# Attention's order of work: copies that follow one another at the rate of issue, and two weight tiles fetched at the head of the stage

## The chip, the cores and the metric

One core of a Trainium2 chip runs the whole model in one launch. The core has a matrix engine (PE, TensorE; its weight loads are shown as PEld), a vector engine (DVE), an activation engine (ACT), GpSimd (POOL) and SyncE (SP), which here mostly issues DMA transfers. Each engine takes its instructions strictly in the order in which the program lists them; engines wait for one another by semaphores. The metric is device time in microseconds for one execution, 2202.79 us before the change, the median of three runs.

## The reference

The input has 1024 tokens of width 1024. Layer 0 mixes tokens with a gated linear recurrence, layer 1 with stick-breaking attention, and each is followed by a SwiGLU feed-forward block. The change touches only the attention of layer 1:

```python
qkv = einsum("bsd,de->bse", rms_norm(h), w_qkv)       # q, k, v of 16 heads of 64
z = einsum("bhqd,bhkd->bhqk", q, k) / 8
log_fail = where(s < t, log_sigmoid(-z), 0)           # strictly earlier keys only
suffix = reversed_cumsum(log_fail) - log_fail
weights = where(s < t, exp(log_sigmoid(z) + suffix), 0)
out = einsum("bhqk,bhkd->bhqd", weights, v) @ w_o     # then the residual and the FFN
```

## The kernel before, in words

Values are float32. Each operand of a matrix product is split into a high part, rounded to the matrix engine's format, and a low part, the remainder; a product is then three matmuls (high by high, low by high, high by low; `mm3`, lines 443 to 446), or two where one side is held exactly.

Attention works on eight pairs of heads, because two heads of 64 fill the 128 partitions. For each pair q there are six projection groups: Q, K and V (`which` = 0, 1, 2), each for the two halves n of the tokens. A group is eight steps `proj` (`project`, line 1709) of three 512-column matmuls each. For Q and K the result is scaled by DVE into `t` (`scaled`, L1723), split by ACT into `qh` (`q_hi`, L1727) and by DVE into `ql` (`q_lo`, L1731), and then copied by DMA to other partitions: `move` (L1746) copies 64 rows by 512 columns, four times for a Q group and eight for a K group. Of the eight copies of a K group, x = 0 to 3 are for the first head (`kh` twice, then `kl` twice) and x = 4 to 7 for the second. A step `z` (`z_part`, L1786) multiplies a 128-token block of Q with `kh` and with `kl`; ACT takes the sigmoid into `F` (L1798), DVE the running product (L1805, L1807). PE transposes the result (`T`, L1817), ACT and DVE split it (L1822, L1826), and PE multiplies it with V (`av`, L1834). V itself is differenced and transposed as `vt` (L1757) and split (L1768, L1772). There are 24 `z` chunks and 24 units of `T` and `av` in a pair; a head's chunks begin with the blocks j = 0 to 3 of the first half and go on with j = 4 to 7, whose diagonal chunks need the second K group (n = 1).

Weights for a projection come from HBM into one of three `raw` buffers (`load_raw`, L425, 512 KB each), and are split by ACT and DVE in two halves (`whi` L1697, `wlo` L1701). All of these transfers, the copies, the weights, the stores `out` of finished heads (L1895) and, for the last pair, the loads `back` of those (L1775) are issued by SP, in one queue.

The order of the instructions on every engine is not written by hand. `attention_plan` (line 191) adds tasks to a `Plan` (line 35), each with an engine, an assumed duration, its dependencies and a rank (a due time in units). `Plan.emit` then runs a list scheduling: it repeatedly takes the ready task that could begin first, the lower rank deciding ties, and emits it. What it assumes of time changes only the order in which instructions are listed; what makes an engine wait in the execution are the real dependencies. A DMA task in the plan keeps the queue for 0.55 and ends after its own duration (line 68):

```python
            if eng == "dma":
                free[eng], end[i] = begin + 0.55, begin + us
```

In the plan before, each copy of a group also depends on the copy before it (`m`), so that eight copies follow one another at the full duration of 2.1 plus 0.15. Nothing in the kernel's data asks for that; SP issues the copies as they come in its list.

Ahead of the plan stands a loop written out by hand (lines 1911 to 1933): it issues the projections (0,0,n) and (0,1,n), that is Q and K of the first pair, and at the head of each weight's first group it loads a further one: weight (0,1) at g = 0, weight (0,2) at g = 2, after the copies of group (0,0,1). The splits of the loaded weight follow PE's steps one by one from the list `later`. The plan begins where this loop ends, with the times of the engines given as `Plan(pe=0.0, dve=1.0, act=1.0, dma=1.0)`.

Of the kernel before, what the change touches and what calls it, by code (L numbers as in the profile page):

```python
# [190 lines left out]
def attention_plan(plan, fn):  # L191
    NP, LEAD = HEADS // 2, 8
# [4 lines left out]
    chunks, units = [], []  # L197
    for q in range(NP):
# [5 lines left out]
        else:  # L204
# [3 lines left out]
            for h in heads:  # L208
                chunks += diag(h, range(4, NT)) + rest(h)
                units += upper(h)  # L210
    mm = lambda n: n / 2400 + 0.008
    act = lambda n: 0.08 + n * 0.00082
    dve = lambda n: 0.07 + n * 0.00103

    wlo, wraw, wuse = {}, {}, {}

    def weights(i, name, r, raw, use):
        ld = plan.add("dma", 2.6, fn["load", name], [raw], r - 4)
        h0 = plan.add("act", 0.5, fn["whi", name, 0], [ld, use], r - 2.5)
        l0 = plan.add("dve", 0.6, fn["wlo", name, 0], [h0], r - 2.3)  # L220
        h1 = plan.add("act", 0.5, fn["whi", name, 1], [h0], r - 2.1)
        wlo[name] = (l0, plan.add("dve", 0.6, fn["wlo", name, 1], [h1, l0], r - 1.9))
        wraw[i] = wlo[name][1]
# [3 lines left out]
    vadd, kept, zlast, avlast, vlow, turn = {}, {}, {}, {}, {}, {}  # L227
    is_kept = lambda q, n: q < NP - 2 + (n == 0)
    order = []
    for i, (q, which, n) in enumerate(groups):  # L230
        s, wi = 24 * (q - 1) + 4 * (i % 6), 3 * q + which
        if i >= 4:
            if n == 0 and wi > 2:
                weights(wi, (q, which), s, wraw.get(wi - 3), wuse.get(wi - 2))
            p = None
            for k in range(ND):
                need = [p, pt.get(i - 2) if k == 0 else None]
                if wi > 2:
                    need.append(wlo[q, which][k // 4])
                p = plan.add("pe", 0.692, fn["proj", q, which, n, k], need, s + k / 2 + 0.5)  # L240
            proj[i] = wuse[wi] = p
        s += 4
        if i < 3:
            continue
        p = proj.get(i)
        if which < 2:
            order.append(i)
            was = order[-3] if len(order) > 2 else None
            pt[i] = plan.add("dve", 0.6, fn["t", q, which, n], [p, moves.get(was)], s + 0.1)
            th = plan.add("act", 0.5, fn["qh", q, which, n], [pt[i], moves.get(was)], s + 0.2)  # L250
            tl = plan.add("dve", 0.6, fn["ql", q, which, n], [th], s + 0.3)
            m = None
            for x in range(4 + 4 * which):
                src = (tl if x % 2 else th) if which == 0 else (tl if x // 2 % 2 else th)
                old = [(zlast, q - 2)] if q > 1 else []
                m = plan.add("dma", 2.1, fn["move", q, which, n, x], [src, m, *old], s + 0.4)
                moved[q, which, n, x // (2 + 2 * which)] = m
            moves[i] = m
        else:
            old = [(vadd, (q - 2, x)) for x in range(2)] if q > 1 else []  # L260
            pt[i] = plan.add("dve", 0.6, fn["t", q, which, n], [p, *old], s + 0.1)
            before = (dv, (q, n - 1) if n else (q - 1, 1)) if q or n else None
            turned = (turn, (q, n - 1) if n else (q - 1, 1)) if q or n else None
            dv[q, n] = plan.add("dve", 0.66, fn["dv", q, n], [pt[i], before, turned], s + 0.4)
            if q == NP - 1:
                m = None
                for y in range(NP - 1 - n):
                    for x in range(2):
                        m = plan.add("dma", 2.4, fn["back", y, n, x], [p, (kept, (y, n)), m], s + 0.5)
                        back[y, n] = m  # L270

    sig, scan, T = {}, {}, {}
    users = {}
    for c, (q, hx, j, ci) in enumerate(chunks):
        s, dg = c - LEAD, j // 4 == ci
        n = (j % 4 + 1) * P if dg else NB
        need = [sig.get(c - 2), moved.get((q, 0, j // 4, hx)), moved.get((q, 1, ci, hx))]
        zlast[q] = zz = plan.add("pe", 2 * mm(n), fn["z", c], need, s)
        if q < NP - 1:
            f = j if dg else j + 4  # L280
        elif dg:
            f = j % 4 + 4 * hx
        else:
            f = j + 4 + 4 * hx
        free = [(T, u) for u in users.get(f, ())] + ([(zlast, NP - 2)] if f >= 12 else [])
        sig[c] = plan.add("act", act(n), fn["sig", c, f], [zz, *free], s + 0.2)
        need = [sig[c], None if dg else scan[q, hx, j, 1]]
        scan[q, hx, j, ci] = plan.add("dve", 0.07 + n * 0.00222, fn["scan", c], need, s + 0.3)
        users[f] = [
            u for u, (q_, hx_, G, kb) in enumerate(units)  # L290
            if (q_, hx_, G) == (q, hx, j // 4) and kb // 4 == ci and kb <= j
        ]

    turns = {}
    for q in range(NP):
        first = [u for u, x in enumerate(units) if x[0] == q]
        turns[max(first[0] - 1, 0)] = (q, 0)
        turns[next(u for u in first if units[u][3] >= 4) - 1] = (q, 1)
    tl, av, ring, banks, sums = {}, {}, [], [], {}
    stored = None  # L300
    for u, (q, hx, G, kb) in enumerate(units):
        if u in turns:
            v = turns[u]
            old = [(avlast, v[0] - 2)] if v[0] > 1 else []
            turn[v] = t = plan.add("pe", 0.45, fn["vt", *v, len(ring)], [dv[v], *ring[-2:-1]], u - 1.9)
            vh = plan.add("act", 0.5, fn["vh", *v], [t, *old], u - 1.8)
            vlow[v] = plan.add("dve", 0.6, fn["vl", *v], [vh], u - 1.7)
            ring.append(vlow[v])
        js = range(max(kb, 4 * G), 4 * G + 4)
        n = len(js) * P  # L310
        need = [scan[q, hx, j, kb // 4] for j in js] + ring[-2:-1]
        T[u] = plan.add("pe", 0.109 * len(js) + 0.02, fn["T", u, len(ring)], need, u - 1.8)
        th = plan.add("act", act(n), fn["th", u], [T[u], av.get(u - 3)], u - 1.6)
        tl[u] = plan.add("dve", dve(n), fn["tl", u], [th], u - 1.5)
        ring.append(tl[u])
        need = [tl[u], av.get(u - 1), (vlow, (q, kb // 4)), *(banks[-2:-1] if kb == 4 * G else ())]
        av[u] = plan.add("pe", 2 * mm(n), fn["av", u, len(banks)], need, u + 0.8)
        if kb != 3:
            continue
        avlast[q] = av[u]  # L320
        s = u + 1
        need = [av[u], sums.get((q, G)) if hx else kept.get((q - 1, G))]
        g0 = plan.add("act", 0.5, fn["g0", q, hx, G], need, s)
        g1 = plan.add("dve", 0.6, fn["g1", q, hx, G], [g0], s + 0.1)
        banks.append(g1)
        sums[q, G] = g1
        if hx == 0:
            continue
        vadd[q, G] = plan.add("dve", 0.66, fn["vadd", q, G], [g1, pt.get(6 * q + 4 + G)], s + 0.5)
        free = stored if is_kept(q, G) else proj[len(groups) - 2 + G]  # L330
        ph = plan.add("act", 0.5, fn["ph", q, G], [vadd[q, G], free], s + 0.6)
        kept[q, G] = plan.add("dve", 0.66, fn["pl", q, G], [ph], s + 0.7)
        if is_kept(q, G):
            stored = plan.add("dma", 2.1, fn["out", q, G, 0], [ph], s + 0.8)
            kept[q, G] = plan.add("dma", 2.1, fn["out", q, G, 1], [kept[q, G], stored], s + 0.9)

    s, out = 24 * (NP - 1), []
    for o in range(4):
        i = 3 * NP + o
        weights(i, f"o{o}", s + 6 * o - 2, wraw.get(i - 3), wuse.get(i - 2) if o < 2 else zlast[NP - 2])  # L340
        p = None
        bank = pt[len(groups) - 2 + o] if o < 2 else out[o - 2]
        for k in range(ND):
            need = [p, bank, wlo[f"o{o}"][k // 4], back[k, 0] if k < NP - 1 else kept[NP - 1, 0]]
            p = plan.add("pe", 0.685, fn["ob", o, k], need, s + 4 * o + k / 2 + 0.6)
        if o < 2:
            out.append(plan.add("act", 0.5, fn["keep", o], [p, pt[len(groups) - 2 + o]], s + 4 * o + 5))
# [4 lines left out]
def trunk(  # L352
# [1309 lines left out]
    with ExitStack() as st:  # L1662
# [201 lines left out]
        def ob_part(o, k):  # L1864
# [2 lines left out]
            product(OB[o], f"o{o}", k, 0)  # L1867

        acts = {
            "load": load,  # L1870
            "whi": w_hi,
            "wlo": w_lo,
# [35 lines left out]
        E = mybir.EngineType  # L1908
        with tc.manual_schedule(engines={E.PE, E.Activation, E.DVE, E.Pool, E.SP}):
            sts, later = stats_steps(), []  # L1910
            for i in range(4 * ND):
                if i >= 5:
                    next(sts, None)
                g, k = divmod(i, ND)
                if k == 0:
# [6 lines left out]
                            move(*was, x)  # L1922
                    if g % 2 == 0:
                        name = (0, g // 2 + 1)
                        load(name)
                        later += [
                            lambda a=name: w_hi(a, 0),
                            lambda a=name: (w_lo(a, 0), w_hi(a, 1)),
# [2 lines left out]
                project(0, g // 2, g % 2, k)  # L1931
                if i >= 5 and later:
                    later.pop(0)()
            plan = Plan(pe=0.0, dve=1.0, act=1.0, dma=1.0)
            chunks, units = attention_plan(plan, Steps(acts))
            plan.emit()
            mix.load(2)
# [59 lines left out]
```

## Time and profile before

| | us |
|---|---|
| median of 3 runs (lowest, highest) | 2202.79 (2198.71, 2205.09) |
| the profiled execution | 2201.81 |
| its span, first to last instruction | 2200.0 |
| attention, from the first projection to the last product of the plan | about 950 to 1480 of the span |
| one pair of heads in the middle of attention | about 61 |

A stretch of the span given as A:B is in microseconds from the first instruction. A row of a timeline gives start, duration, engine, line and what is written and read; in brackets, where there is one, the engine's idle time before it and what ended that. For SP the duration of a merged row also holds its waits. The duration of a matmul row holds its passage through the array; the distance from one start to the next tells how fast they follow.

### The profile page before, as it was taken

To read this page: it belongs to the slowest core of one execution; us is meant where nothing else is said; L and a number is where in the kernel's file an instruction comes from. 1 tells how busy PE (TensorE), PEld (TensorE's weight loads), DVE (VectorE), ACT (ScalarE), POOL (GpSimd) and SP (SyncE) were. 2 spreads that over 40 slices of the span, in tenths; PEclk is the share of its full clock that TensorE was granted. 3 is DMA by queue.
4 is the path that set the end of the run, shared out by engine and by line. 5 is a ranking of instruction groups with operands and counts; after the bars stand their busy time and mean duration, and the time that the engine had idled before them with its cause. 6 is when DMAs were issued, how large, how long until landed. Compare 5 with 4: busy or idle time off the path is not lost.

```text
span 2200.0 us, 27262 instructions
## 1 busy us (share of the span) xinstructions
PE 2167.9 (99%) x10054; PEld 1798.9 (82%) x10054; DVE 1709.1 (78%) x2434; ACT 1078.5 (49%) x1776; POOL 35.6 (2%) x44
## 2 busy tenths in 40 slices
PE   9999999999999999989999999999999999999997
PEld 7888888888888888868888888888888888888886
DVE  7978678677777887957888888877876777788886
ACT  5577444444444554644555555544534444454455
POOL 0000010000000000000000000002000000000001
PEclk9999999999999999989999999999999999999999
DMA  4111312344444864433333333442133444466442
GB/s 174 39 48 48 125 39 91 98 138 139 150 146 130 286 197 129 128 102 108 99 94 94 91 101 97 136 178 88 58 115 117 149 136 149 153 236 225 134 138 87
DMA packets 132598, 274.50 MB, mean 125 GB/s; under 512 B 15344, under 2 KB 22640, under 8 KB 132464
## 3 DMA queue, kind: packets, MB, share of 16 engines
q1 hardware_dynamic: 132032, 271.97, 38.9%
q8 instruction: 79, 1.29, 0.2%
q10 hardware_dynamic: 432, 0.79, 0.1%
q14 instruction: 55, 0.45, 0.1%
HBM read 176.75 MB, written 70.78 MB: 113 GB/s over the span
## 4 chain that ended last, share of the span: by engine, by line
PE 90%; DVE 5%; ACT 2%; DMA 2%; issue 1%; SPq 0%; DVEq 0%; ACTq 0%
PE p_ps L446 18%; PE p_ps L444 18%; PE p_ps L445 18%; PE qk_ps L444 3%; PE qk_ps L445 3%; PE qk_ps L446 3%; PE z_ps L1786 3%; PE a_ps L445 3%; PE a_ps L444 3%; PE a_ps L446 3%; PE av_ps L1834 3%; PE wt_ps L1817 2%; PE ob_ps L444 2%; PE ob_ps L445 2%; PE ob_ps L446 2%; DMA kl<-ql 2%
## 5 line engine op out<-in xcount | busy, mean ns | idle before, releaser
L444 PE MATMUL p_ps<-vh,wbh 128*128 128x512 f32 x524 | 204.9, 391 | 2.0 <-ACT ta L1362 2.0
L446 PE MATMUL p_ps<-vh,wbl 128*128 128x512 f32 x524 | 204.8, 391 | 0.0
L446 PE MATMUL p_ps<-vh,wcl 128*128 128x512 f32 x524 | 204.1, 390 | 0.5 <-DVE wcl L977 0.5
L445 PE MATMUL p_ps<-vl,wbh 128*128 128x512 f32 x524 | 204.6, 390 | 0.0
L446 PE MATMUL p_ps<-vh,wal 128*128 128x512 f32 x524 | 204.1, 389 | 0.1
L444 PE MATMUL p_ps<-vh,wch 128*128 128x512 f32 x524 | 204.1, 389 | 0.0
L445 PE MATMUL p_ps<-vl,wch 128*128 128x512 f32 x524 | 203.9, 389 | 0.0
L445 PE MATMUL p_ps<-vl,wah 128*128 128x512 f32 x524 | 203.9, 389 | 0.0
L444 PE MATMUL p_ps<-vh,wah 128*128 128x512 f32 x524 | 203.8, 389 | 0.0
L1798 ACT ACTIVATE F<-z_ps 128x512 f32<-128x512 f32 (+3 forms) x188 | 91.8, 490 | 168.3 <-PE z_ps L1786 167.2
L963 ACT CAST wbh<-sb 128x1024 fp32r<-128x1024 f32 (+2 forms) x69 | 69.6, 1008 | 192.6 <-DVE sb L947 192.6
L1805 DVE TENSOR_TENSOR_SCAN F<-F,unit 128x128 f32<-128x128 f32 (+3 forms) x128 | 104.8, 821 | 62.9 <-ACT F L1798 62.7
L444 PE MATMUL qk_ps<-vh,whi 128*128 128x512 f32 x264 | 119.4, 452 | 0.7 <-ACT vh L524 0.7
L444 PEld LDWEIGHTS p_ps<-vh,wbh 128*128 128x128 f32 x524 | 98.7, 188 | 22.7 <-ACT ta L1362 2.5
L446 PEld LDWEIGHTS p_ps<-vh,wbl 128*128 128x128 f32 x524 | 98.8, 189 | 21.9 <-DVE wbl L967 1.3
L446 PEld LDWEIGHTS p_ps<-vh,wcl 128*128 128x128 f32 x524 | 98.4, 188 | 21.8 <-DVE wcl L977 1.3
L446 PEld LDWEIGHTS p_ps<-vh,wal 128*128 128x128 f32 x524 | 98.4, 188 | 21.3 <-DVE wal L958 1.0
L445 PEld LDWEIGHTS p_ps<-vl,wbh 128*128 128x128 f32 x524 | 98.7, 188 | 20.4
L445 PEld LDWEIGHTS p_ps<-vl,wah 128*128 128x128 f32 x524 | 98.4, 188 | 20.4
L445 PEld LDWEIGHTS p_ps<-vl,wch 128*128 128x128 f32 x524 | 98.4, 188 | 20.4
L444 PEld LDWEIGHTS p_ps<-vh,wah 128*128 128x128 f32 x524 | 98.4, 188 | 20.3
L444 PEld LDWEIGHTS p_ps<-vh,wch 128*128 128x128 f32 x524 | 98.4, 188 | 20.3
(375 smaller groups left out, 5494.5 us busy)
## 6 DMA issues: line engine op xcount, KB each, us to landing
raw<-in_ffn_w_in SPq DMA_DIRECT2D x88, 512.0 KB, 3.6
vl<-pd SPq DMA_DIRECT2D x128, 256.0 KB, 3.6
pd<-U SPq DMA_DIRECT2D x90, 256.0 KB, 2.3
raw<-in_ffn_w_out SPq DMA_DIRECT2D x28, 512.0 KB, 4.1
raw<-in_attn_w_qkv SPq DMA_DIRECT2D x24, 512.0 KB, 4.4
kh<-qh SPq DMA_DIRECT2D x64, 128.0 KB, 2.3
kl<-ql SPq DMA_DIRECT2D x64, 128.0 KB, 2.7
acc<-pd SPq DMA_DIRECT2D x28, 256.0 KB, 2.6
```

The lines of the kernel that those rows point to most:

```text
L444: nc.tensor.matmul(ps, lhsT=wh, rhs=mh, start=first, stop=False, **kw)
L445: nc.tensor.matmul(ps, lhsT=wh, rhs=ml, start=False, stop=False, **kw)
L446: nc.tensor.matmul(ps, lhsT=wl, rhs=mh, start=False, stop=last, **kw)
L963: nc.scalar.copy(self.full(self.wb), self.full(self.sb))
L1786: nc.tensor.matmul(ps[:, 0:n], lhsT=lhsT, rhs=rhs, start=i == 0, stop=i == 1)
L1798: nc.scalar.activation(F, Z.pop(c)[:, 0:n], AF.Sigmoid, scale=-SC)
L1805: V.tensor_tensor_scan(rev, rev, unit[:, NB - n :][:, ::-1], 0.0, op0=ALU.mult, op1=ALU.add)
L1817: nc.tensor.transpose(tp[:, c : c + P], F[:, (kb % 4) * P : (kb % 4 + 1) * P], ident)
L1834: nc.tensor.matmul(ps[:, c:], lhsT=VV[q][:, kb, hx], rhs=t.pop(u)[:, c:], start=kb == 4 * G and i == 0, stop=kb == 3 and i == 1,)
```

## The change

The change keeps every instruction of the computation and alters what the planner assumes and two places of the hand-written loop.

1. In the plan, copies (`move`), stores (`out`) and loads (`back`) no longer depend on the copy ahead of them, and take 2.4 instead of 2.1. `moved`, `moves` and `back` hold lists, so that what uses a group depends on all its copies.
2. The plan's duration of a weight load is 4.8 instead of 2.6, a projection step 0.705 instead of 0.692, and the constant of a matmul 0.015 instead of 0.008.
3. The transposes `vt` of V are due one unit later.
4. The first K group's copies, made ahead of the plan, are no longer taken as there at once, but at 1.3 and 3.7 (`clock0`, `clock1`, tasks that emit nothing); DVE and ACT start at 0.5 instead of 1.0, the DMA queue at 1.3.
5. In the loop ahead of the plan, the loads of weights (0,1) and (0,2) are both issued at its head. The splits stay where they were.

```diff
@@ attention_plan
-    mm = lambda n: n / 2400 + 0.008
+    mm = lambda n: n / 2400 + 0.015
...
-        ld = plan.add("dma", 2.6, fn["load", name], [raw], r - 4)
+        ld = plan.add("dma", 4.8, fn["load", name], [raw], r - 4)
...
+    for hx in range(2):
+        moved[0, 1, 0, hx] = [plan.add(f"clock{hx}", 1.3 + 2.4 * hx, fn["wait", 0])]
...
-                p = plan.add("pe", 0.692, fn["proj", q, which, n, k], need, s + k / 2 + 0.5)
+                p = plan.add("pe", 0.705, fn["proj", q, which, n, k], need, s + k / 2 + 0.5)
...
-            m = None
+            old = [(zlast, q - 2)] if q > 1 else []
             for x in range(4 + 4 * which):
                 src = (tl if x % 2 else th) if which == 0 else (tl if x // 2 % 2 else th)
-                old = [(zlast, q - 2)] if q > 1 else []
-                m = plan.add("dma", 2.1, fn["move", q, which, n, x], [src, m, *old], s + 0.4)
-                moved[q, which, n, x // (2 + 2 * which)] = m
-            moves[i] = m
+                m = plan.add("dma", 2.4, fn["move", q, which, n, x], [src, *old], s + 0.3 + x / 100)
+                moved.setdefault((q, which, n, x // (2 + 2 * which)), []).append(m)
+                moves.setdefault(i, []).append(m)
...
             if q == NP - 1:
-                m = None
                 for y in range(NP - 1 - n):
-                    for x in range(2):
-                        m = plan.add("dma", 2.4, fn["back", y, n, x], [p, (kept, (y, n)), m], s + 0.5)
-                        back[y, n] = m
+                    back[y, n] = [
+                        plan.add("dma", 2.4, fn["back", y, n, x], [p, (kept, (y, n))], s + 0.5 + y / 10) for x in range(2)
+                    ]
...
-        turns[max(first[0] - 1, 0)] = (q, 0)
-        turns[next(u for u in first if units[u][3] >= 4) - 1] = (q, 1)
+        turns[first[0]] = (q, 0)
+        turns[next(u for u in first if units[u][3] >= 4)] = (q, 1)
...
-            stored = plan.add("dma", 2.1, fn["out", q, G, 0], [ph], s + 0.8)
-            kept[q, G] = plan.add("dma", 2.1, fn["out", q, G, 1], [kept[q, G], stored], s + 0.9)
+            stored = plan.add("dma", 2.4, fn["out", q, G, 0], [ph], s + 0.8)
+            kept[q, G] = plan.add("dma", 2.4, fn["out", q, G, 1], [kept[q, G]], s + 0.9)
@@ trunk, ahead of the plan
             sts, later = stats_steps(), []
+            load((0, 1))
+            load((0, 2))
...
                         name = (0, g // 2 + 1)
-                        load(name)
...
-            plan = Plan(pe=0.0, dve=1.0, act=1.0, dma=1.0)
+            plan = Plan(pe=0.0, dve=0.5, act=0.5, dma=1.3, clock0=0.0, clock1=0.0)
```

More of the change, by code (lines that the diff above doesn't have):

```diff
@@ L248, in attention_plan @@
             was = order[-3] if len(order) > 2 else None
-            pt[i] = plan.add("dve", 0.6, fn["t", q, which, n], [p, moves.get(was)], s + 0.1)
-            th = plan.add("act", 0.5, fn["qh", q, which, n], [pt[i], moves.get(was)], s + 0.2)
+            pt[i] = plan.add("dve", 0.6, fn["t", q, which, n], [p, *moves.get(was, ())], s + 0.1)
+            th = plan.add("act", 0.5, fn["qh", q, which, n], [pt[i], *moves.get(was, ())], s + 0.2)
             tl = plan.add("dve", 0.6, fn["ql", q, which, n], [th], s + 0.3)
-            m = None
+            old = [(zlast, q - 2)] if q > 1 else []
             for x in range(4 + 4 * which):
                 src = (tl if x % 2 else th) if which == 0 else (tl if x // 2 % 2 else th)
-                old = [(zlast, q - 2)] if q > 1 else []
-                m = plan.add("dma", 2.1, fn["move", q, which, n, x], [src, m, *old], s + 0.4)
-                moved[q, which, n, x // (2 + 2 * which)] = m
-            moves[i] = m
+                m = plan.add("dma", 2.4, fn["move", q, which, n, x], [src, *old], s + 0.3 + x / 100)
+                moved.setdefault((q, which, n, x // (2 + 2 * which)), []).append(m)
+                moves.setdefault(i, []).append(m)
         else:
@@ L276, in attention_plan @@
         n = (j % 4 + 1) * P if dg else NB
-        need = [sig.get(c - 2), moved.get((q, 0, j // 4, hx)), moved.get((q, 1, ci, hx))]
+        need = [sig.get(c - 2), *moved.get((q, 0, j // 4, hx), ()), *moved.get((q, 1, ci, hx), ())]
         zlast[q] = zz = plan.add("pe", 2 * mm(n), fn["z", c], need, s)
@@ L343, in attention_plan @@
         for k in range(ND):
-            need = [p, bank, wlo[f"o{o}"][k // 4], back[k, 0] if k < NP - 1 else kept[NP - 1, 0]]
+            need = [p, bank, wlo[f"o{o}"][k // 4], *(back[k, 0] if k < NP - 1 else [kept[NP - 1, 0]])]
             p = plan.add("pe", 0.685, fn["ob", o, k], need, s + 4 * o + k / 2 + 0.6)
@@ L1869, in trunk @@
         acts = {
+            "wait": lambda _: None,
             "load": load,
```

## The prediction

> **What bounds the kernel now.** I read the page first, then stretches of attention, then PE's waits there, then timelines at the places that these name.
>
> ```profile
> span 2200.0 us, 27262 instructions
> ...
> PE 2167.9 (99%) x10054; PEld 1798.9 (82%) x10054; DVE 1709.1 (78%) x2434; ACT 1078.5 (49%) x1776; POOL 35.6 (2%) x44
> ...
> PE 90%; DVE 5%; ACT 2%; DMA 2%; issue 1%; SPq 0%; DVEq 0%; ACTq 0%
> ```
>
> PE is busy for 99% of the span and makes 90% of the chain that ended last. The change removes no matmul, so it can only win back time in which PE waits, or add to it.
>
> ```profile
> core 0: us, PE busy (x) PEld busy (x) DVE busy (x) ACT busy (x) POOL busy (x), PEclk, DMA share, GB/s
> 982.47:991.41 8.94, 3.94 (x11) 3.08 (x11) 3.06 (x6) 2.69 (x4) 0.00 (x0) 0.62 0.62 139
> 1121.00:1182.00 61.00, 59.91 (x322) 50.42 (x321) 50.92 (x77) 31.51 (x66) 0.10 (x1) 1.00 0.35 96
> 1182.00:1243.00 61.00, 59.38 (x320) 49.99 (x319) 50.43 (x76) 31.54 (x66) 0.10 (x1) 1.00 0.35 95
> 1420.00:1440.00 20.00, 20.00 (x111) 16.70 (x110) 18.67 (x31) 12.15 (x26) 0.00 (x0) 1.00 1.01 335
> ```
>
> The first row is the passage from the hand-written loop to the plan: PE works 3.94 of 8.94 us, at a granted clock of 0.62. The next two are about one pair of heads each: PE lacks 1.1 and 1.6 us, and DVE with some 50 of 61 is not the bound. The last row is in the final pair: the transfer engines are full (1.01), and PE still never stops. PE's waits between 945 and 1465, by total, number and longest:
>
> ```profile
> PE z_ps L1786 <- DMA kl<-ql: 8.3, 8, 1.6
> PE z_ps L1786 <- DMA kh<-qh: 4.4, 1, 4.4
> ...
> PE z_ps L1786 <- ACT F L1798: 0.5, 1, 0.5
> ```
>
> Nine waits, 12.7 us, are for copies of K. Inside the planned part PE waits for ACT or DVE only once, 0.5 us.
>
> **The change, part by part.** *The entry (weight (0,2) loaded at the head, `clock` tasks).* PE, SP, ACT and DVE around the passage:
>
> ```profile
> 982.24 0.39 PE L446 MATMUL qk_ps<-vh,wlo 128*128 128x512 f32 x1
> 987.01 0.44 PE L1786 MATMUL z_ps<-kh,q 128*128 128x128 f32 x1 [4.38 <-DMA kh<-qh]
> 988.07 0.44 PE L1786 MATMUL z_ps<-kl,q 128*128 128x128 f32 x1 [0.62 <-DMA kl<-ql]
> ...
> 988.85 0.63 PE L445 MATMUL qk_ps<-vl,whi 128*128 128x512 f32 x1
> 989.28 0.63 PE L446 MATMUL qk_ps<-vh,wlo 128*128 128x512 f32 x1
> ...
> 991.70 0.40 PE L445 MATMUL qk_ps<-vl,whi 128*128 128x512 f32 x1
> 991.93 0.39 PE L446 MATMUL qk_ps<-vh,wlo 128*128 128x512 f32 x1
> ```
>
> ```profile
> 976.87 0.58 SPq L425 DMA_DIRECT2D raw<-in_attn_w_qkv  x1
> 983.84 1.10 SPq L1746 DMA_DIRECT2D kh<-qh  x2
> ...
> 988.84 1.55 SPq L425 DMA_DIRECT2D raw<-in_attn_w_qkv  x3
> 990.49 1.11 SPq L1746 DMA_DIRECT2D kh<-qh  x2
> ```
>
> ```profile
> 980.57 1.14 ACT L1697 CAST whi<-raw 128x512 fp32r<-128x512 f32 x2 [7.36 <-DMA raw<-in_attn_w_qkv]
> ```
>
> ```profile
> 981.23 1.29 DVE L1701 TENSOR_TENSOR wlo<-raw,whi 128x512 fp32r<-128x512 f32 x2 [7.29 <-ACT whi L1697]
> 982.44 0.68 DVE L1723 TENSOR_TENSOR t<-qk_ps,rbc 128x512 f32<-128x512 f32 x1
> ```
>
> The weight (0,2) is issued at 976.87, because SP has to pass the copies of Q first. ACT stands 7.36 us before it, DVE 7.29 us before ACT, and behind both, in order, wait the scaling and split of K's first group. That group's scaling starts at 982.44. Its matmuls were over one group earlier: 24 matmuls at the 0.23 between 991.70 and 991.93 are 5.5 us, so at 982.47 - 5.5 = 977.0. PE finishes the second group at 982.47 (0.23 after its last start) and finds no K.
>
> After the change the load is SP's second instruction of the stage. What it needs is the third buffer, which the feed-forward stage reads last here, and SP's queue:
>
> ```profile
> 941.18 0.33 SPq L425 DMA_DIRECT2D raw<-in_attn_w_qkv  x1
> ```
>
> ```profile
> 945.70 0.43 DVE L978 TENSOR_TENSOR wcl<-raw,wch 128x256 fp32r<-128x256 f32 x1
> ```
>
> It can leave at 946.1 at the latest of these two. SP may stand there for up to 4.6 us with stores of the residual behind it; nothing in attention uses SP before Q's copies, over 20 us later, so this costs nothing. The splits stay at their place behind PE's step 16 (about 972) and wait for no transfer. Then K's scaling starts at about 977.2, its first copy 1.4 later as in the rows (982.44 to 983.84), at 978.6; the fourth copy has landed 4.2 after the first was issued (983.84 to 988.07), at 982.8. The `clock` tasks hold the first `z` until 1.3 in the plan, so PE lists three projection steps of V ahead of it (3 x 0.69, to 984.5): no wait.
>
> What it saves: in 982.47 to 991.41 PE did six projection matmuls (6 x 0.23 = 1.4) and `z` of 128 and 256 columns, each twice (in proportion 0.06 and 0.115, together 0.35). 8.94 - 1.75 = 7.2 us, of which 5.0 are the two waits and the rest the distance of 0.43 instead of 0.23 after them. The 1.62 us wait below, in the stretch 1182:1243, shows a clock of 1.00.
>
> [...]
>
> *What is late next.* The plan finds two weight loads ready at 1.3 and the second K group's copies not before 1.9 (scaling to 1.1, `qh` to 1.75, 0.15 on top), so two 512 KB loads are listed ahead of these copies, the third behind them. Landing times of three loads in a row from 988.84, of the copies behind them at 990.49, and of the copies at 983.84 that had a free queue:
>
> ```profile
> DMA to landing us min/median/max: 4.0/5.2/6.4
> ```
>
> ```profile
> DMA to landing us min/median/max: 6.0/6.1/6.2
> ```
>
> ```profile
> DMA to landing us min/median/max: 2.2/2.3/2.3
> ```
>
> SP needs 5.0 for eight copies (983.84 to 988.84), so after the change the loads leave at 983.6 and 984.2; the second lands at 984.2 + 5.2 = 989.4, and four copies behind it, at an estimated 0.4 each, at 991. The fifth chunk, `z` of block 4, needs them. In PE's list it stands behind eight projection steps (5.5) and four chunks (1280 columns, twice: 1.15), so PE is there at 989.1 and waits 1.8. The ends are 0 (the plan puts the chunk a group later) and 3.6 (copies issued until 986.6 take the 6.1 of the second landing row). I take 1.8, which is worked out from the nearest rows.
>
> *The copies without a chain.* In a later pair, PE, SP and DVE, and the landing of the copy issued at 1235.94:
>
> ```profile
> 1234.47 0.39 PE L1786 MATMUL z_ps<-kl,q 128*128 128x512 f32 x1
> 1239.02 0.22 PE L1786 MATMUL z_ps<-kh,q 128*128 128x128 f32 x1
> 1240.86 0.30 PE L1786 MATMUL z_ps<-kl,q 128*128 128x128 f32 x1 [1.62 <-DMA kl<-ql]
> ```
>
> ```profile
> 1229.44 1.10 SPq L1746 DMA_DIRECT2D kh<-qh  x2
> ...
> 1235.56 0.34 SPq L425 DMA_DIRECT2D raw<-in_attn_w_qkv  x1
> 1235.94 0.46 SPq L1746 DMA_DIRECT2D kl<-ql  x1
> ```
>
> ```profile
> 1227.98 0.68 DVE L1723 TENSOR_TENSOR t<-qk_ps,rbc 128x512 f32<-128x512 f32 x1
> ```
>
> ```profile
> DMA to landing us min/median/max: 4.8/4.8/4.8
> ```
>
> The waiting 128-column chunk is again block 4, the first user of K's second group. That group's copies begin at 1229.44, but the plan spaces them at 2.25, interleaved with the rest of the first group. The fourth leaves 6.5 us after the first, directly behind a weight load, takes 4.8 to land instead of 2.3, and PE waits. Without the chain the four leave 0.6 apart, by about 1231.5, and land by 1234; behind a weight load by 1236.5. Chunks are due about 2.5 us apart, so after 1234.3 block 4 is due at about 1237: no wait. All K waits but those of the entry, 8.3 - 0.62 = 7.7 us in seven places, go. DVE and ACT have no more to do, and the other half of the copies only comes earlier.
>
> *Loads `back` and stores `out`.* In 1420:1440 PE is full while the transfers are at 1.01; the unchained loads for the first token half can only leave sooner, those of the second wait for their projection. Cost 0. If cover failed, it would be by one load's landing there, under 6 us; I count none.
>
> *Durations and due times.* The real step is 3 x 0.23 = 0.69; the plan now holds 0.705. PE then comes earlier than planned by 0.015 x 48 steps = 0.7 us a pair, and may meet operands that ACT or DVE have not finished: 0 to 5 us over seven pairs. The one wait of 0.5 above speaks for the low end; I take 1. `vt` one unit later has two units (5 us) before its first use; 0, covered by that distance. The 4.8 for a weight load moves only splits, which are due later than that.
>
> **Sum.** -7.2 - 7.7 + 1.8 + 1.0 = -12.1 us. The profiled execution took 2201.81 (span 2200.0 and 1.8 around it) and becomes 2189.7; it lies 1.0 below the median, so the median becomes 2190.7.
>
> **The rivals.** *Slower: the plan trusts 2.4 us, the queue gives 6.1.* Where copies stand behind weights, PE is led to `z` 3.7 us too early (6.1 - 2.4). The chain, for all its cost, was slack for exactly that. Once per pair, over seven pairs, this is 25.9 - 14.9 = +11, 2213.8; it decides from 14.9 / 7 = 2.1 us a pair. For it: the landing rows. Against it: in the pair shown, one load stands in some 16 copies, the margin of block 4 is about 3 us without it, and PE waited at no other chunk.
> [...]
>
> *The pairs keep their waits.* If weights still fall between the first and fourth copy, or DVE's split comes late, only the entry is won: -7.2 + 1.8 + 1.0 = -4.4, 2198.4. For it: K waits stand in all pairs; against: their one visible cause is the spacing.
>
> *The planner's pace.* ACT and DVE late everywhere at the upper end: -14.9 + 1.8 + 5 = -8.1, 2194.7. The single 0.5 speaks against it.
>
> *It does not do what it says*: SP still reaches the load late, and the lists hardly differ: 2202.8. The load ahead of it, already at 941.18, speaks against that.
>
> **How the numbers follow.** Forecast 0.66, own range 2186 to 2197; slower 0.13; waits kept 0.10; pace 0.08; no effect 0.03. About 0.3% (6.6 us) is what a measurement can tell from none: below 2196.2 is faster. Faster: 0.64 of the forecast and 0.07 of the pace, 0.71; same: the rest of these two, kept waits and no effect, 0.16; slower 0.13. The range 2186 to 2200 holds the forecast, the pace and the kept waits, about 0.8; its low end is all 14.9 gained and nothing lost (2187.9), with 2 for the scatter of the runs.
>
> **What would show it.** Right: `whi` of (0,2) waits for no transfer; the first `z` follows within 3 us of the last K matmul, with no stretch at half clock; block 4's wait of the first pair is 1 to 3 us; the other K waits sum to under 1; a pair takes 59 to 60 us. Wrong: new waits of PE for `kh` or `kl` behind weight loads, waits for `F`, `tl` or `vl` above 0.5 a pair, or waits at `ob`.

## The result and the profile after

The changed kernel takes 2186.59 us (median of 5 runs, 2183.76 to 2191.96) against 2204.13 us (5 runs, 2198.71 to 2207.08): a ratio of 0.9927, 95% interval 0.9906 to 0.9947, so faster by 11.7 to 20.7 us. 2190.7 had been predicted. The profiled execution took 2188.74 us, 13.1 less than the one of before.

The page of the changed kernel, its span and busy times:

```profile
span 2187.0 us, 27244 instructions
...
PE 2165.4 (99%) x10054; PEld 1797.8 (82%) x10054; DVE 1707.1 (78%) x2434; ACT 1078.3 (49%) x1776; POOL 35.6 (2%) x44
```

The same number of matmuls, nearly the same busy time, 13.0 us less span: time was won where PE waited. PE's waits inside attention (945 to 1480; total, number, longest), above 0.5 us:

```profile
PE z_ps L1786 <- DMA kl<-ql: 2.7, 2, 2.0
PE qk_ps L445 <- DVE vl L525: 0.7, 1, 0.7
PE qk_ps L444 <- ACT vh L524: 0.6, 1, 0.6
PE wt_ps L1817 <- DVE tl L1826: 0.6, 1, 0.6
```

Of the nine waits for copies of K (12.7 us) none is left; the two for `kl` here, 2.7 us, are new and stand in the first pair. The other three rows were there before too, and the one wait for `F` (0.5 us) is gone. The stretch from the fourth to the fifth pair's first product with V has become

```profile
1180.99:1240.70 59.71, 59.71 (x321) 50.41 (x320) 50.66 (x77) 31.60 (x67) 0.10 (x1) 1.00 0.36 98
```

(length, then busy PE, PEld, DVE, ACT, POOL; clock, DMA share, GB/s): PE is busy for all of it. To see where the time went I cut each profile at the starts of five kinds of rows: the last matmul of K's first projections, the first product with V (L1834) in the pairs 0, 6 and 7, and the last one. The stretches between these cuts in us, for most of the profiles that follow:

| profile | up to K | entry | six pairs | next pair | last pair | rest | span |
|---|---|---|---|---|---|---|---|
| before | 982.2 | 23.9 | 366.3 | 59.5 | 45.7 | 722.4 | 2200.0 |
| before, again | 979.6 | 25.0 | 368.8 | 59.3 | 45.6 | 721.1 | 2199.4 |
| changed | 980.9 | 21.2 | 358.1 | 59.5 | 45.1 | 722.3 | 2187.0 |
| changed, again | 979.6 | 18.8 | 358.1 | 59.5 | 45.1 | 722.1 | 2183.1 |
| loads early, old plan | 980.0 | 16.8 | 368.8 | 59.5 | 45.6 | 721.3 | 2191.9 |
| new plan, loads late | 980.7 | 25.2 | 358.1 | 59.5 | 45.1 | 722.3 | 2190.9 |
| only the copies unchained | 982.3 | 25.2 | 357.3 | 63.6 | 45.6 | 721.2 | 2195.3 |
| changed, next loads behind | 981.0 | 16.5 | 358.1 | 59.5 | 45.1 | 722.0 | 2182.2 |
| changed, old durations | 979.6 | 20.8 | 357.4 | 63.0 | 45.1 | 722.3 | 2188.1 |

**The entry.** SP, ACT and PE of the changed kernel at the passage to the plan:

```profile
941.43 0.33 SPq L425 DMA_DIRECT2D raw<-in_attn_w_qkv  x1
...
946.40 0.33 SPq L425 DMA_DIRECT2D raw<-in_attn_w_qkv  x1
...
977.25 1.10 SPq L1746 DMA_DIRECT2D kh<-qh  x2
...
982.24 1.08 SPq L425 DMA_DIRECT2D raw<-in_attn_w_qkv  x2
983.41 1.11 SPq L1746 DMA_DIRECT2D kh<-qh  x2
984.62 1.20 SPq L1746 DMA_DIRECT2D kl<-ql  x2
```

```profile
971.73 1.14 ACT L1697 CAST whi<-raw 128x512 fp32r<-128x512 f32 x2
```

```profile
980.86 0.39 PE L446 MATMUL qk_ps<-vh,wlo 128*128 128x512 f32 x1
...
982.89 0.39 PE L446 MATMUL qk_ps<-vh,wlo 128*128 128x512 f32 x1
983.12 0.22 PE L1786 MATMUL z_ps<-kh,q 128*128 128x128 f32 x1
...
990.13 0.30 PE L1786 MATMUL z_ps<-kh,q 128*128 128x128 f32 x1 [1.99 <-DMA kl<-ql]
991.13 0.30 PE L1786 MATMUL z_ps<-kl,q 128*128 128x128 f32 x1 [0.70 <-DMA kl<-ql]
...
993.60 0.63 PE L444 MATMUL qk_ps<-vh,whi 128*128 128x512 f32 x1
994.03 0.63 PE L445 MATMUL qk_ps<-vl,whi 128*128 128x512 f32 x1
```

Weight (0,2) leaves at 946.40 instead of 976.87, ACT splits it at 971.73 with no wait, and K's first copy leaves 3.6 us before the last K matmul (980.86 in this profile) instead of 1.6 after it. The first `z` follows the projections without a gap. Then two weight loads pass ahead of the copies of K's second group, and block 4 waits 1.99 and 0.70, after which PE runs at 0.43 instead of 0.23 from matmul to matmul for some 3 us.

### The profile page after: what moved, and what is told of

Same layout as the page of the kernel before. It is cut to its first block, busy times and chain, and to the rows that moved or that the text cites. A ratio compares the mean times of both kernels' runs of the same rounds, so it can differ in the third digit from the quotient of the medians.

```text
span 2187.0 us, 27244 instructions
## 1 busy us (share of the span) xinstructions
PE 2165.4 (99%) x10054; PEld 1797.8 (82%) x10054; DVE 1707.1 (78%) x2434; ACT 1078.3 (49%) x1776; POOL 35.6 (2%) x44
## 3 DMA queue, kind: packets, MB, share of 16 engines
q8 instruction: 79, 1.29, 0.2%
## 4 chain that ended last, share of the span: by engine, by line
PE 94%; DVE 3%; ACT 2%; DMA 0%; issue 0%; SPq 0%; DVEq 0%; ACTq 0%
PE p_ps L446 18%; PE p_ps L444 18%; PE p_ps L445 18%; PE qk_ps L444 4%; PE qk_ps L446 4%; PE qk_ps L445 4%; PE z_ps L1786 3%; PE av_ps L1834 3%; PE wt_ps L1817 3%; PE a_ps L445 3%; PE a_ps L446 3%; PE a_ps L444 3%; PE ob_ps L445 2%; PE ob_ps L444 2%; PE ob_ps L446 2%; PE g_ps L446 1%
## 5 line engine op out<-in xcount | busy, mean ns | idle before, releaser
L446 PEld LDWEIGHTS p_ps<-vh,wal 128*128 128x128 f32 x524 | 98.3, 188 | 21.2 <-DVE wal L958 1.0
```

What stands on the lines that cost most here:

```text
L446: nc.tensor.matmul(ps, lhsT=wl, rhs=mh, start=False, stop=last, **kw)
```

## The experiments

**Both kernels once more.** No edit; the changed kernel:

> The changed kernel once more, on the same chip as the next three, so that they can be compared with it. Its first profiled execution had a span 13.0 us shorter than before: 1.4 by the end of K's first projections (where a stretch of half clock was shorter, at a place that the change does not touch), 2.7 from there to the first product with V, 8.2 over the six pairs that follow, 0.6 at the end. If the stretch of half clock ahead of the change varies from execution to execution, this gain lies between 11.5 and 17; if it belongs to the change, it stays near 13 or above in every execution.

2186.09 us (2184.95 to 2187.11), ratio 0.9930 (0.9918 to 0.9943), 15.2 us under its own runs of before, inside the 11.5 to 17 expected. And the kernel before:

> The kernel before, profiled once more. The stretch 957 to 966, ahead of everything that the change touches, had a granted clock of 0.62 in the profile of before, 0.81 in that of the changed kernel and 1.00 in its repetition. Theory: this varies from one execution to the next in the same kernel and is no part of the gain, so the clock there comes out anywhere between 0.6 and 1.0 here; the nine waits for copies of K are there again, 12 to 13 us. Rival: the early weight load does something to that stretch; then it is 0.62 again, as before.

2200.46 us (2199.34 to 2201.86); its nine waits for copies of K are there again, 13.6 us in all, a little above the 12 to 13 expected. The granted clock is the last but two of a window's columns. The stretch 957 to 966 stands ahead of everything that the change touches but the early load; its window in before, before again and changed:

```profile
957.00:966.00 9.00, 9.00 (x39) 7.93 (x38) 3.40 (x13) 1.56 (x5) 0.72 (x4) 0.62 0.00 0
```

```profile
957.00:966.00 9.00, 8.90 (x51) 7.27 (x50) 5.18 (x18) 2.35 (x6) 0.72 (x4) 1.00 0.00 0
```

```profile
957.00:966.00 9.00, 9.00 (x45) 7.62 (x45) 4.78 (x17) 1.80 (x5) 0.72 (x4) 0.81 0.00 0
```

0.62 and 1.00 for one and the same kernel: this clock varies from execution to execution. The 1.4 us that the first two profiles differ up to K need not be the change's; the second two do not differ there. In the second pair of profiles (979.6 both) the difference of the spans is 16.3 us: 6.2 at the entry, 10.7 in the six pairs, 0.5 in the last, and 1.0 lost behind attention. The two profiles of before differ there by 1.3 too (722.4 and 721.1), so that loss is not shown to be the change's. The six pairs of before came out 2.5 us longer than the first time: one pair took 63.25 instead of 61. Its wait for K, and the stretch that holds it with the next one:

```profile
1300.76 0.30 PE L1786 MATMUL z_ps<-kl,q 128*128 128x128 f32 x1 [1.88 <-DMA kl<-ql]
```

```profile
1298.30:1301.71 3.41, 1.53 (x12) 1.26 (x11) 0.93 (x3) 0.60 (x2) 0.00 (x0) 1.00 0.91 236
1301.71:1305.12 3.41, 3.41 (x12) 2.83 (x11) 2.12 (x4) 1.24 (x3) 0.00 (x0) 0.50 0.00 0
```

A wait of 1.88 us, and a clock of 0.50 for the 3.41 us from 1301.71, which costs an estimated 1.7 us more (half of 3.41). So the waits that the change takes away cost more than their length, in some executions.

**The loads alone,** on the kernel before.

```diff
             sts, later = stats_steps(), []
+            load((0, 1))
+            load((0, 2))
...
-                        load(name)
```

> Before, with only the two weight loads at the head of the stage; the plan and its chained copies are those of before. Theory: the two parts are separate, so the entry's waits (4.4 and 0.6 us and the half clock behind them) go and the waits of the pairs (1.1 to 1.6 each) stay: 6 to 7 us faster than before, ratio 0.997. Rival: the entry's gain needs the new plan too (its clocks for the first K copies), since the old plan lists the first z at once; then under 3 us.

2193.50 us (2191.49 to 2197.34), ratio 0.9967 (0.9954 to 0.9979), 7.8 us under its own runs of before, where 6 to 7 had been expected. The entry is 16.8 us, 7.1 and 8.2 less than in the two profiles of before; one wait of 0.17 for a copy is left there, and the pairs keep theirs (8.4 us in all). The part is separate, as the theory had it; the rival falls.

**The plan alone,** from the changed kernel.

```diff
-            load((0, 1))
-            load((0, 2))
...
+                        load(name)
```

> The changed kernel with the two weight loads put back to where they were (the first at the head, the second behind the copies of Q). Theory: the six pairs gain the full 8.2 us, and the entry keeps its wait for the first copies of K (about 3 us, since three steps of V now stand ahead of it, with half clock behind it) and has the wait at block 4 on top: 7 to 9 us faster than before, ratio 0.9960 to 0.9968. Rival: the gain of the pairs needs the early load too; then under 4 us.

2191.69 us (2190.58 to 2192.84), ratio 0.9962 (0.9950 to 0.9975). The six pairs are 358.1, all of the pairs' gain. The entry has both sets of waits:

```profile
985.19 0.30 PE L1786 MATMUL z_ps<-kh,q 128*128 128x128 f32 x1 [1.46 <-DMA kh<-qh]
986.24 0.45 PE L1786 MATMUL z_ps<-kl,q 128*128 128x128 f32 x1 [0.76 <-DMA kl<-ql]
993.96 0.30 PE L1786 MATMUL z_ps<-kh,q 128*128 128x128 f32 x1 [1.56 <-DMA kl<-ql]
995.02 0.30 PE L1786 MATMUL z_ps<-kl,q 128*128 128x128 f32 x1 [0.77 <-DMA kl<-ql]
```

The expectation of about 3 us for the first copies was too high: the three steps of V that the new plan lists ahead leave 1.46 and 0.76 of the 4.38 and 0.62 of before. 9.4 us here and 7.8 with the loads alone are 17.2, and both together gave 15.2. The 2.0 between lie within the intervals of these ratios (each some 2.7 us either way). One overlap is seen in the rows: what the plan alone saves of the entry's first waits, some 2.8 us, cannot be won a second time when the loads take these waits away altogether.

**Only the chain of the copies taken out** of the kernel before (with the lists that this needs; each copy also gets the 2.4 and its own rank).

```diff
-                m = plan.add("dma", 2.1, fn["move", q, which, n, x], [src, m, *old], s + 0.4)
+                m = plan.add("dma", 2.4, fn["move", q, which, n, x], [src, *old], s + 0.3 + x / 100)
```

> Before, with only the chain between the copies of a group taken out of the plan (2.4 each, ranks in their order); loads, durations, due times, stores, loads back and clocks as before. Theory: this one edit makes the pairs 59.7 us instead of 61.05, 8 us over six pairs, and leaves the entry's 5 us of waits and the half clock behind them; the old load duration of 2.6 adds a wait of up to 3.5 in the last pair: 4 to 8 us faster than before. Rival: the new durations and due times are needed for the pairs; then they stay above 60.5.

2195.43 us (2193.48 to 2197.61), ratio 0.9978 (0.9969 to 0.9987). The six pairs are 357.3, 59.55 each: this one edit is the pairs' gain. But the next pair is 63.6 instead of 59.5, which was the caveat in the expectation; the versions under "Durations and due times" go after it.

**The second pair's loads behind the copies,** in the changed kernel.

```diff
-                weights(wi, (q, which), s, wraw.get(wi - 3), wuse.get(wi - 2))
+                weights(wi, (q, which), s, wraw.get(wi - 3, moves[3][-1]), wuse.get(wi - 2))
```

> The changed kernel, with the weight loads of the second pair listed only behind the last copy of the first pair's second K group (in the plan these three loads depend on that copy). Theory: the two waits of PE at block 4 of the first pair (2.0 and 0.7 us) and the half clock behind them are made by the two 512 KB loads ahead of the copies, so they go: 4 to 5 us faster than the changed kernel, and the copies land 2.3 us after their issue. Rival: the copies are late because the split of K's second group is late; then the waits stay near 2.

2183.17 us (2182.89 to 2183.99), ratio 0.9919 (0.9905 to 0.9932); 2.9 us under the changed kernel on the same chip, 2184.95 to 2187.11 there, and less than the 4 to 5 expected. SP and PE at the entry, and the copies' landing (of the `kl` copies in 982:990):

```profile
982.85 1.10 SPq L1746 DMA_DIRECT2D kh<-qh  x2
984.05 1.18 SPq L1746 DMA_DIRECT2D kl<-ql  x2
...
987.84 8.25 SPq L425 DMA_DIRECT2D raw<-in_attn_w_qkv  x4
```

```profile
988.11 0.22 PE L1786 MATMUL z_ps<-kh,q 128*128 128x128 f32 x1
988.17 0.28 PE L1786 MATMUL z_ps<-kl,q 128*128 128x128 f32 x1
```

```profile
DMA to landing us min/median/max: 2.2/2.3/2.3
```

The copies of the changed kernel, issued from 983 to 985.9 behind two loads, by contrast:

```profile
DMA to landing us min/median/max: 5.6/5.9/6.1
```

They left at about the same time and took 3.6 us longer. The loads ahead of them made the new wait; the split was not late. At the entry this version is 4.7 and 2.3 us shorter than the two profiles of the changed kernel, the first of which had the half clock behind its waits; the 4 to 5 had been taken from that one. All four of its runs lie below all five of the changed kernel's.

**Durations and due times.** Four versions on the changed kernel: all the old values, only the old load duration, only the old due times of `vt`, and (on the version with the loads behind) only the old steps and matmuls. The first two edits stand in the first and the last version, the third in the first two, the others in the first and third:

```diff
-    mm = lambda n: n / 2400 + 0.015
+    mm = lambda n: n / 2400 + 0.008
-                p = plan.add("pe", 0.705, fn["proj", q, which, n, k], need, s + k / 2 + 0.5)
+                p = plan.add("pe", 0.692, fn["proj", q, which, n, k], need, s + k / 2 + 0.5)
...
-        ld = plan.add("dma", 4.8, fn["load", name], [raw], r - 4)
+        ld = plan.add("dma", 2.6, fn["load", name], [raw], r - 4)
...
-        turns[first[0]] = (q, 0)
+        turns[max(first[0] - 1, 0)] = (q, 0)
-        turns[next(u for u in first if units[u][3] >= 4)] = (q, 1)
+        turns[next(u for u in first if units[u][3] >= 4) - 1] = (q, 1)
```

> The changed kernel with the old durations of a step, a matmul and a weight load (0.692, 0.008, 2.6) and the old due times of vt. Theory: only the chain of the copies mattered for the pairs; within 1.5 us of the changed kernel, pairs of 59.7 us. The rival of the planner's pace: the slower plan costs PE waits for ACT and DVE; then the pairs get shorter here by up to 0.7 us each, 5 in all.

2190.01 us (2186.55 to 2190.86), ratio 0.9944 (0.9931 to 0.9958): slower than the changed kernel by about 4, not within 1.5. The pairs are 59.56 instead of 59.7: the new durations cost 0.8 us in six pairs, though PE shows no wait in those pairs in either kernel. The loss is one wait with half clock behind it; PE, the clock around it, and ACT's wait between 1395 and 1430:

```profile
1413.03 1.05 PE L1817 MATMUL wt_ps<-ident,F 128*128 128x128 f32 x4 [1.88 <-DVE v L1772]
```

```profile
1409.73:1413.14 3.41, 1.53 (x8) 1.03 (x7) 1.44 (x3) 2.77 (x6) 0.00 (x0) 1.00 1.05 401
1413.14:1416.55 3.41, 3.41 (x11) 2.84 (x12) 3.41 (x6) 0.58 (x1) 0.00 (x0) 0.50 1.06 392
```

```profile
ACT kl L1697 <- DMA raw<-in_attn_w_o: 3.6, 1, 3.6
```

ACT stands before a weight of the output projection that has not landed; the split of V behind it comes late, and PE waits. 1.9 of wait and an estimated 1.7 by the half clock (half of 3.41) are the 3.5 us. The changed kernel's repetition has the row of ACT too, but short:

```profile
ACT kl L1697 <- DMA raw<-in_attn_w_o: 0.2, 1, 0.2
```

The kernel before has it with 1.8 us (1.5 in its second profile), and PE does not wait behind it there.

> The changed kernel with only the old duration of a weight load (2.6) in the plan. Theory: with 2.6 the plan lists the split of a weight on ACT before it has landed; ACT then stands 3.6 us before it in the last pair, and PE waits about 1.9 us for the split of V and runs at half clock for a while: the stretch from the seventh to the eighth pair's first product with V is 63 us instead of 59.5, 3.5 us over the changed kernel in all. Rival: the due time of vt made that wait; then 59.5 here.

> The changed kernel with only the old due times of vt (one unit earlier). Theory: no effect, 59.5 us from the seventh to the eighth pair and 59.7 in the others. Rival: the wait in the last pair appears here; then 63 us.

2188.17 us (2187.55 to 2191.85), ratio 0.9940 (0.9923 to 0.9957), and 2186.63 (2185.53 to 2191.67), ratio 0.9932 (0.9917 to 0.9948): by their times alone neither can be told from the changed kernel's 0.9930. ACT's wait in each:

```profile
ACT kl L1697 <- DMA raw<-in_attn_w_o: 3.0, 1, 3.0
```

```profile
ACT kl L1697 <- DMA raw<-in_attn_w_o: 2.2, 1, 2.2
```

The next pair is 60.9 with the old load duration and 60.6 with the old due times, instead of 59.5: each alone lengthens the wait of ACT (3.0 and 2.2) and costs 1.5 and 1.1 us, neither the 3.5. PE's wait behind it is 1.26 and 0.86, and the clock stays at 1.00 (1400 to 1425). I had expected the 3.5 of the load duration alone, and nothing of `vt`; both were wrong.

> The changed kernel with the second pair's weight loads behind the copies (the 2183.2 us version) and with the old durations of a step and of a matmul (0.692, 0.008), but the new 4.8 for a weight load and the new due times of vt. Theory: the old durations alone took 0.13 us off each pair, and the 3.5 us wait in the last pair came from the old load duration, which is not in here: 0.8 us faster than that version, 2182 to 2183. Rival: the wait in the last pair comes from the step durations or from vt; then 2185 to 2187, with PE waiting about 2 us for the split of V.

2181.33 us (2180.70 to 2184.57), ratio 0.9919 (0.9905 to 0.9933); its next pair is 59.3, so the steps' durations do not make that wait. Five of its six pairs are 59.5. Its ratio to before is that of the version with the new steps, and they ran on different occasions, so which of the two is faster is open.

**Loads put ahead of the copies** of the changed kernel, one or three.

```diff
         def move(q, which, n, x):
...
+            if which == n == 1 and x == 2 and q:
+                for e in extra:
+                    nc.sync.dma_start(e, w_qkv[q])
             nc.sync.dma_start(f32(dst)[to, cs], f32(t)[src])
```

> The changed kernel, with one further transfer of 512 KB (a weight tile copied inside HBM, its result unused) issued in the pairs 1 to 7 just ahead of the two kl copies that block 4 of the second K group needs. In the changed kernel these copies land about 2.4 us before block 4 uses them. Theory: 2.4 us is the margin that was left, and one load ahead puts off a landing by about 2.5 us as in before (4.8 instead of 2.3) and the issue by 0.4: a wait of PE of 0 to 1.2 us a pair, 0 to 8 us over the changed kernel's 2186. Rival (slower): one load ahead already costs 3.7 us a pair; 2212 and above.

2191.48 us (2191.22 to 2192.68), 5.4 above the changed kernel's repetition. PE's waits for `kl` are 4.6 us in six places, two of them the entry's; in the pairs they are 0.4 to 1.0. Of the 5.4, 4.0 are lost in the six pairs; 1.8 are lost in the next pair, where ACT stands 2.9 us before a weight of the output projection and PE waits 1.6 for the split of V. The expectation had only the copies in mind.

> The same with three such transfers in a row. Theory: with a transfer taking some 1.8 us of the queue, as three weight loads in a row did, the copies land about 5.8 us late, PE waits about 3.4 us a pair and runs at half clock for a while behind it (up to 2 us more): 24 to 36 us over the changed kernel, 2210 to 2222, slower than before. If the queue does not work in order of issue, the copies overtake and the time stays near that with one.

2227.97 us (2225.36 to 2231.89), ratio 1.0122 (1.0107 to 1.0137): slower than before, and 6 us above the range expected. Waits of PE in attention, and one of them with the matmuls behind it:

```profile
PE z_ps L1790 <- DMA kl<-ql: 25.9, 8, 4.3
```

```profile
1247.43 0.30 PE L1790 MATMUL z_ps<-kl,q 128*128 128x128 f32 x1 [4.15 <-DMA kl<-ql]
...
1248.74 0.63 PE L445 MATMUL qk_ps<-vl,whi 128*128 128x512 f32 x1
1249.17 0.63 PE L446 MATMUL qk_ps<-vh,wlo 128*128 128x512 f32 x1
```

The `kl` copies that left at 1239.95 landed 6.8 us later, against 2.3 on a free queue: they did not overtake the three transfers ahead of them. With three loads ahead a copy landed late enough to make the change a loss. With one (4.1 to 4.5 in the pair at 1222), block 4's margin is just used up.

## Why the prediction was right, point by point

*The entry, -7.2.* Right: 7.1 and 8.2 by the loads alone, by the mechanism given (ACT and DVE free of the wait for the weight, K's copies ahead of PE's end).

*The new wait at block 4, +1.8.* Right in place and cause: block 4 of the first pair behind two 512 KB loads, undone by listing them behind. Mis-sized in two ways. The landing of the fourth copy, forecast at 991, is 8.5 us behind the end of K's projections; it was 10.0 in the first profile (981.09 to 991.13) and 9.2 in the repetition. The estimate of 0.4 for each copy behind the second load came from no row; the 5.6 to 6.1 measured from issue to landing are near the 6.1 of the prediction's second landing row, which it used only for the upper end. The waits are 2.7 in one execution and 1.8 in the other. The second error is what follows: with the half clock behind it, it cost 4.7 (21.2 - 16.5) in the first. The sum counts a wait of 1.8 at its own length alone. Of the two profiles only the repetition shows that (1.21 and 0.62, the clock of 989 to 992 at 1.00); in the first the clock was 0.50 from 992.12 to 995.53.

*The copies, -7.7.* Right, by the chain alone as its one cause. Taking out the chain alone gives -9.0 against the first profile of before (366.3 to 357.3) and -11.5 against the second; with the new durations it is -8.2 and -10.7. In the first profile of before the clock was 1.00 from 995 to 1470, so the excess of 1.3 is not the half clock there. An idle time in brackets counts from the end of the row before, and a row outlasts the distance to the next by some 0.16 (0.39 against 0.23), so six waits cost about 1.0 more than their brackets; the rest is open. In the second profile one stretch of half clock adds an estimated 1.7 (half of 3.41).

*The planner's pace, +1.0.* Near in size, but the mechanism was not seen: 0.8 in six pairs with the new steps and matmuls, and no wait of PE on ACT or DVE in those pairs with either. What costs the 0.8 stays open.

*Loads `back` and stores `out`, 0.* Not a cost, and perhaps a gain: the last pair is 45.1 in every version with the new plan and 45.6 in those without, the copies alone included; the one wait for `F` of before is gone in it. No run takes this edit by itself.

*Durations of loads and `vt`, 0.* This step failed in its reasoning though not in the sum. I called both covered by distance. Taking the chain out without them exposes a wait for a weight of the output projection in the seventh pair (63.6 instead of 59.5); the new load duration and the new due time together keep it short. They are worth up to 3.5 us in the new plan, about half of it by the half clock (the estimated 1.7), and nothing in the old one, where that stretch was 59.5.

*The sum.* -12.1 against -13.1 in the profiles first compared, -15.2 in the medians of the repetition, -17.5 in the first medians. That the first is so near is in part luck: at the entry -5.4 was forecast and -2.7 came, in the six pairs -6.7 and -8.2, and the 1.4 up to the end of K's projections and the 0.6 in the last pair were in no term. In the second pair of profiles the entry is -6.2 and the six pairs are -10.7. What the sum leaves out is the half clock, which makes a wait dearer in some executions, in the kernel before and in the changed one; beyond that, the stretch up to the end of K's projections, with a clock of 0.62 to 1.00 at 957 to 966, differs by up to 2.7 us between profiles (979.6 to 982.3).

*The rivals.* The slower one names a real mechanism, shown with extra loads (copies that landed 6.8 us after their issue): but in the changed kernel only the entry has two loads ahead of the needed copies. In the later pairs none stands there (the copies from 1221.5 to 1226.5 of one pair run through, the load is at 1228), so it was not reached. That the pairs keep their waits, or that nothing changes, is refuted by the pairs of 59.7 us.

## What to carry to other kernels

The planner's wrong assumption about transfers showed here as short, regular waits of PE, the busiest engine, at one and the same consumer (7.7 us in seven places): look at which transfer it is, when it was issued and what stands ahead of it in the queue, before changing the consumer. When copies and large loads share a queue, list a load behind the copies that something needs soon; a copy of 128 KB took 2.3 us alone and 5.9 behind two loads of 512 KB. And when an assumption in such a planner is mended, check the others with it: unchaining the copies alone was worth 5.6 us here, the whole of the new plan 9.4.

## What the runs showed of the hardware

PE's clock dropped to 0.50 after waits of 1.99 and 0.70 us within 3.0 us (changed kernel) and behind a single one of 1.88 (before, again), but stayed at 1.00 after 1.62 (before). In the repetition the same place had waits of 1.21 and 0.62 and kept its spacing of 0.23, with a clock of 1.00 from 989 to 992:

```profile
988.05 0.30 PE L1786 MATMUL z_ps<-kh,q 128*128 128x128 f32 x1 [1.21 <-DMA kl<-ql]
988.97 0.30 PE L1786 MATMUL z_ps<-kl,q 128*128 128x128 f32 x1 [0.62 <-DMA kl<-ql]
...
990.07 0.39 PE L445 MATMUL qk_ps<-xg,whi 128*128 128x512 f32 x1
990.29 0.39 PE L446 MATMUL qk_ps<-xg,wlo 128*128 128x512 f32 x1
```

In the profile of before the clock was 1.00 to 984.65 and 0.50 from 984.70, so it fell 2.1 us into the wait of 4.38, which began at 982.63.

The cases differ in where a wait lies. In the profiles of before and of the changed kernel the stretches of half clock begin whole multiples of 3.41 us apart (957.37 and 984.68 in before, eight of them; 957.99 and 992.12 in the changed kernel, ten) and last 3.41 us or twice that, but for the last, which lasts 5.6. Divided at these places, the changed kernel around its new waits, and before around its 1.62:

```profile
988.71:992.12 3.41, 1.29 (x6) 1.09 (x7) 0.90 (x3) 0.28 (x1) 0.00 (x0) 1.00 1.06 254
992.12:995.53 3.41, 3.41 (x11) 2.72 (x10) 2.54 (x5) 0.38 (x1) 0.00 (x0) 0.50 0.29 95
```

```profile
1237.28:1240.69 3.41, 1.96 (x10) 1.41 (x8) 1.95 (x4) 0.59 (x1) 0.00 (x0) 1.00 0.99 267
1240.69:1244.10 3.41, 3.24 (x20) 2.93 (x21) 2.32 (x4) 1.74 (x4) 0.00 (x0) 1.00 0.16 40
```

2.1 of 3.41 us idle, and the next stretch has half the clock; 1.45 idle, the rest of the wait falling into the next stretch, and it keeps the full clock. In the stretches ahead of the falls at 1301.71 (before, again) and 1413.14 (changed, old durations), shown above, 1.88 are idle. From 976 to 1510 in the profiles of before and of the changed kernel, each divided in this way, the full clock fell twice, behind 2.04 and 2.12 us of idle time, and it stayed behind every stretch with 1.45 or less. This is read from these four falls alone, and it does not cover the falls near 957, which came behind 1.32 (before) and 1.29 (changed). A wait of 1.62 us thus cost here its own length alone, and one of 1.88 an estimated 1.7 us more (half of 3.41). That the place of a wait between these borders decides is the author's reading of these cases; the borders lie elsewhere in each of the two profiles.

The clock differs between executions of one kernel at the same place (0.62 and 1.00 at 957 to 966 in the two profiles of before), and with no change in it the stretch up to the end of K's projections took 982.2 in the one and 979.6 in the other.
